# Two-place attention loads, branch sums in the other buffer, and a planner that counts accumulating transfers by other constants, in an encoder layer on one Trainium2 core

## The chip, the core and the metric

The kernel runs on one core of a Trainium2 chip. Time is device time of one execution in microseconds (us); lower is better. TensorE (PE) does the matmuls, VectorE (DVE) and ScalarE (ACT) the element-wise work, GpSimd (POOL) a few scalings and the accumulating transfers, and SyncE (SP) issues nearly all other transfers (DMAs). The five engines run their own instruction queues in order and wait for each other by semaphores. The profile also gives the clock that was granted to TensorE, as a share of full speed.

## The reference

One post-norm layer over 1024 frames of width 1024, float32 in and out:

```
proj = x @ w_in                                  # q,k,v (8 heads of 64), f_a, q_b,f_b,i_b,g_b, two gates
y_a = fox_attention(q, k, v, log_sigmoid(f_a))   # causal softmax(q.k/8 + F[t] - F[s]) @ v
y_b = rms_norm(hgrn2(silu(q_b), 1-f, i_b, log f)) * norm_g * sigmoid(g_b)   # linear recurrence
merged = sigmoid(gate_a) * (y_a @ w_pa) + sigmoid(gate_b) * (y_b @ w_pb)
x = layer_norm(ALPHA * x + merged @ w_o)
x = layer_norm(ALPHA * x + (silu(x @ w_g) * (x @ w_u)) @ w_ff_out)
```

## The kernel before

Float32 products are made from three matmuls of split operands (high by high, high by low, low by high), and the large products are cut by a Strassen-like scheme into seven block products p1 to p7. A matmul has 128 rows of weights and mostly 512 columns.

The layer runs in this order: the projections for v, the pairs of q/k and recurrence projections ("b" and "q" in the table ORDER), the recurrence heads ("r"), the early part of the gate projections ("e", products p3 and p7, parked in DRAM as `part_d`), the eight attention heads ("a") interleaved with the late parts of the eight gate pairs ("g"), then the two branch projections with the gates (`pps`), the output projection, the first norm, the feed-forward part and the second norm.

**Planner.** No engine's order is written by hand. The program is recorded call by call, ORDER giving the sequence of the large steps. A planner (class `Plan`) then simulates the engines with costs per instruction and searches for the order with the earliest end; that order is what each engine's queue holds on the chip. `cost` gives a transfer on SP its time from its bytes: 350 bytes per ns, but 235 where the SBUF side has 64 rows, and 220 where the first step of the source is 0. A transfer that POOL issues gets `LANDS` plus its bytes over `RATE` until it lands, and holds the modelled DMA for half of the latter part.

**Attention loads.** In `qk_load` a head's q and k come from DRAM (`qk_d`, split parts hi and lo) into three tiles of 128 rows: q2 holds 64 rows of hi above 64 rows of lo, k2 the hi part twice, kl the lo part twice. That is six transfers of 64 rows, 256 KB each. In `attention` a head's probabilities for late queries lie in a wide tile, in buffer m for even heads and buffer v for odd ones (`take("mv"[i], ...)`); POOL scales them by the reciprocal sums, TensorE transposes them (tile `pt`), ACT and DVE split the transposes (`th`, `tl`), and products with v are summed in `pv`, copied to `ya` and stored to `ya_d`.

**Branch sums.** After attention each of the four chunks (c = 0 to 3, heads 2c and 2c+1) of attention's output is fetched from `ya_d` in `branch_raw`: two heads, hi and lo, 64 rows each. Two plain loads on SP, then two accumulating transfers on POOL that add the lo part to what has landed. The chunks lie in `ybox[0]`, which is buffer v, so they wait for head 7's wide tile; sums and differences of them lie in `ybox[1]`, buffer m. ACT and DVE then split them into the operands y11, y12, y22, ys1 to ys4 of `pps`.

**Late gates.** `gate_late(n)` makes p1, p2, p6, p5, p4 with two PSUM banks, both of the group "h", so gate n+1's second product needs the bank that gate n's p4 leaves. That one is freed by a DVE addition `gl_b<-gl_h,gl_b`, whose second input is the parked p7 of gate n, loaded from `part_d` and used by one more addition before it.

Of the kernel before, what the change touches and what calls it, by code (L numbers as in the profile page):

```python
# [12 lines left out]
ALU = mybir.AluOpType  # L13
# [3 lines left out]
P = 128  # L17
S = 1024
D = 1024
KC = D // P  # L20
NT = S // P
HA, DH = 8, 64
# [8 lines left out]
FIRST = 8  # L31
WARM = 7
ROUNDS = 36
ORDER = ("b10 00", "b20 21", "b11 01", "r0", "q0", "b12 02", "r1", "b22 23", "q1", "r2", "b13 03", "q2", "e0", "r3", "q3", "e1",
         "e2", "e3", "e4", "e5", "e6", "e7", "a0", "a1", "g0", "a2", "a3", "g1", "a4", "g2", "a5", "a6", "g3", "a7", "g4", "g5", "g6", "g7")
MARGIN = 1.06
SLACK = 400.0
SWITCH = 300.0
# [23 lines left out]
class Plan:  # L62
# [2 lines left out]

    LAT = {"PE": 197.0, "ACT": 131.0, "DVE": 128.0, "POOL": 66.0, "SP": 2400.0}
    OWN = {"PE": 0.0, "ACT": 0.0, "DVE": 127.0, "POOL": 60.0, "SP": 2400.0}
    SOFT, LANDS, RATE = 950.0, 1050.0, 190.0
    SETS = {AF.Exp: 0, AF.Ln: 0, AF.Sigmoid: 1, AF.Silu: 2}

    def __init__(self, tc):
# [68 lines left out]
    def cost(self, eng, method, outs, ins, kw):  # L140
        o = outs[0]
        n = o.free_size()
        psum = any(str(a.space).endswith("PSUM") for a in ins)
        if eng == "PE":
            dt = ins[0].dtype
            if method == "transpose":
                return 109.0
            if dt == F32:
                return 2 * max(112.0, n / 1.2 + 2)
            return n / 2.4 + 13.4 if n > 128 else 111.0  # L150
        if eng == "ACT":
            d = n / 1.2 + (52 if psum else 94) + 95 * (o.partition_size() == DH)
            if "accum_out" in kw:
                d += 93
            return d + 93 * sum(isinstance(kw.get(x), bass.AP) for x in ("scale", "bias"))
        if eng == "DVE":
            scal = sum(1 for a in ins if a.free_size() == 1 and n > 1)
            two = method in ("tensor_scalar", "tensor_copy") and not psum
            if method == "reciprocal":
                return 90.0  # L160
            if method == "tensor_tensor_scan":
                return n * 2.1 + 69
            if method == "copy_predicated":
                return n * 1.3 + 69
            if method == "bn_stats":
                n = ins[0].free_size()
            return n * (0.5208 if two else 1.0417) + 69 + 61 * min(scal, 2)
        if eng == "POOL":
            if method == "dma_start":
                return self.SOFT  # L170
            if method == "tensor_tensor" and kw.get("op") == ALU.pow:
                return 500 + 260 * n
            if method == "tensor_scalar":
                return n * 0.833 + 244
            return n * 2.35
        near = ins[0] if str(o.space).endswith("DRAM") else o
        rate = 235.0 if near.partition_size() == DH else 220.0 if ins[0].ap[0][0] == 0 else 350.0
        return float(o.nbytes()) / rate

    def kind(self, call):  # L180
# [2 lines left out]
    def schedule(self, slack, wait):  # L183
# [13 lines left out]
        dma_free = 0.0  # L197
# [18 lines left out]
        while done < len(calls):  # L216
            best = None
            for q, av in avail.items():
                for i in av:
                    t = max(free[q], ready[i])  # L220
                    ok = True
                    need = {}
                    for name in calls[i][6]:
# [10 lines left out]
                        t = max(t, sorted(slots[tag])[k][0] + 60)  # L234
# [3 lines left out]
                    if self.lands[i]:  # L238
                        t = max(t, ring[-RING])
                    if q == "SP":  # L240
                        t = max(t, under_way[-8])
# [8 lines left out]
            t, _, i, q = best  # L250
            c = calls[i]
            avail[q].remove(i)
            d = c[7] * (1 if q in ("PE", "SP") else MARGIN)
# [3 lines left out]
            if q == "SP":  # L257
                start = max(t + 100, dma_free)
                dma_free = start + d
                free[q] = t + 480  # L260
                fin = dma_free
                under_way.append(fin + self.LAT["SP"])
            else:
                if q == "ACT":
                    kind = self.kind(c)
                    if kind is not None and kind != table:
                        table = kind
                        t -= wait
                        d += 1283
                free[q] = t + d  # L270
                fin = t + d + self.lands[i]
                if self.lands[i]:
                    fin += max(0.0, dma_free - t - d)
                    dma_free = max(dma_free, t + d) + 0.5 * (self.lands[i] - self.LANDS)
                    fin = max(fin, ring[-1] + self.lands[i] - self.LANDS)
                    ring.append(fin)
            self.times[i] = t
# [117 lines left out]
def trunk(ctx: ExitStack, tc, a: dict, out: bass.AP):  # L395
# [21 lines left out]
    def take(tag, shape, name, dt=F32):  # L417
        return plan.tile(root, [P] + shape, dt, tag, name, BUFS[tag])
# [26 lines left out]
    def f(ap):  # L445
        return ap.bitcast(F32)
# [91 lines left out]
    b11 = block(0, 0, ("kb", "kb"), "b11")  # L538
# [15 lines left out]
    for k, b, A, p, o in ((0, b11, A11, "p1", vx), (1, b21, A12, "p2", vy)):  # L554
        T = stationary4("v" + p)
        raw = rows(b)
# [160 lines left out]

    ya_d = dram.tile([4, 2, 2, DH, S], F32, name="ya_d")

    v_d = dram.tile([HA, P, NT, 2, DH], F32, name="v_d")  # L720
    for h in range(HA):
        two = take("qk", [NT, 2, DH], f"v{h}", F32R)
# [164 lines left out]
    def qk_load(h):  # L887
        p, i = divmod(h, 2)
        me = slice(i * DH, (i + 1) * DH)
        q2, k2, kl = full("qk", f"q2_{h}", F32R), full("kb", f"k2_{h}", F32R), full("kb", f"kl_{h}", F32R)  # L890
        for t, ns in ((q2, (0, 1)), (k2, (2, 2)), (kl, (3, 3))):
            for j, n in enumerate(ns):
                sync.dma_start(f(t)[j * DH:(j + 1) * DH], qk_d[p, n, me])
        return q2, k2, kl

    def attention(h):
# [251 lines left out]

    ZTAGS = ["kb"] * 4 + ["hl"] * 2 + ["qk"] * 2
    YTAGS = ["qk"] * 4 + ["pf"] * 4  # L1150
    ybox = [take(t, [4, S], f"ybox{t}") for t in "vm"]
    def operand(tag, name):
        t = take(tag, [2, 4, NB], name, F32R)
        return t[:, 0], t[:, 1]
# [20 lines left out]
    def branch_raw(i, c):  # L1175
        if i:
            return raw_load(yb_d[c], [S], f"yr{i}{c}")
        raw = ybox[0][:, c]
        for n in range(2):
            for j in range(2):  # L1180
                o = raw[j * DH:(j + 1) * DH]
                if n:
                    pool.dma_start(o, ya_d[c, j, n], accum_op=ALU.add)
                else:
                    sync.dma_start(o, ya_d[c, j, n])
        return raw

    def gated(i, fb, hf):
# [16 lines left out]
    for c in range(2):  # L1205
# [4 lines left out]
        t = y24[c]  # L1210
# [617 lines left out]
    return np.concatenate([t[:, :1], t[:, 1:, ::-1]], axis=1).reshape(S, D)  # L1828


def _layout(x, w_in, b_fgate, hgrn_lb_logits, hgrn_norm_g, w_branch_a, w_branch_b, w_out, ln1_g, ln1_b,
            w_ff_in, w_ff_out, ln2_g, ln2_b):
    c = np.ascontiguousarray
    x = _backwards(np.asarray(x)[0])
    w = np.asarray(w_in)[0]
    off = np.cumsum([0, 512, 512, 512, HA, 512, 512, 512, 512, D, D])

    def cols(i):
        return w[:, off[i]:off[i + 1]]

    def blocks(m):
        k, n = m.shape
        return m.reshape(k // P, P, n // P, P).transpose(2, 1, 0, 3)

    def pairs(m):
        k, n = m.shape
        return m.reshape(k // (2 * P), 2, P, n // NB, NB).transpose(3, 0, 2, 1, 4)

    def quarters(m):

        k, n = m.shape
        q = m.reshape(k // (2 * P), 2, P, 2, NB).transpose(1, 3, 0, 2, 4).reshape(4, k // (2 * P), P, NB)
        odd = q.shape[1] % 2
        q = np.concatenate([q, np.zeros_like(q[:, :odd])], axis=1)
        return c(q.reshape(4, -1, 2, P, NB).transpose(0, 1, 3, 2, 4))

    wff = np.asarray(w_ff_in)[0]
    return {
        "xT": c(x.T.reshape(KC, P, S)),
        "x": c(x),  # L1860
        "w_v": c(np.stack([cols(i).reshape(2, 4, P, NB) for i in (2, 6)], axis=1)),
        "w_f": c(cols(3).reshape(KC, P, HA).transpose(1, 0, 2)),
        "w_qk": c(np.stack([blocks(cols(0)), blocks(cols(1))])),
        "w_b": c(np.stack([blocks(cols(4)), blocks(cols(5)), blocks(cols(7))])),
        "w_g": c(np.stack([blocks(cols(8)), blocks(cols(9))])),
        "w_p": c(np.stack([blocks(np.asarray(v)[0]).reshape(4, 2, P, 4, P).transpose(0, 2, 1, 3, 4)
                           for v in (w_branch_a, w_branch_b)])),
        "w_o": c(pairs(np.asarray(w_out)[0])),
        "w_ff": c(np.stack([blocks(wff[:, :FF]), blocks(wff[:, FF:])], axis=1)),
        "w_fo": quarters(np.asarray(w_ff_out)[0]),  # L1870
        "bf": c(np.repeat(np.asarray(b_fgate)[0], NT).reshape(NT * HA, 1)),
        "lbl": c(np.asarray(hgrn_lb_logits)[0].reshape(HB, P).T),
        "ng": c(np.asarray(hgrn_norm_g)[0].reshape(P, 1)),
        "ln1c": c(np.concatenate([np.asarray(v)[0].reshape(KC, P).T for v in (ln1_g, ln1_b)], axis=1).reshape(P, 2, KC)),
        "ln1_g": c(np.asarray(ln1_g)[0]), "ln1_b": c(np.asarray(ln1_b)[0]),
        "ln2_g": c(np.asarray(ln2_g)[0]), "ln2_b": c(np.asarray(ln2_b)[0]),
    }
# [17 lines left out]
```

## Time and profile before

| what | value |
|---|---|
| median of 3 runs | 1408.5 us (1408.06 to 1409.1) |
| the profiled execution, its own time | 1405.97 us |
| its span, first to last instruction | 1404.1 us |
| TensorE busy | 1386.7 us, 99% |
| VectorE, ScalarE, GpSimd busy | 1151.3, 659.3, 97.6 us |
| granted TensorE clock, mean | 0.996 |
| moved by DMA | 252.51 MB, mean 180 GB/s |

All views are of the one profiled execution. "Waits" lists who waited for whom: total, number of times, longest. "Windows" gives for each stretch of the span the busy time of PE, PE's weight loads, DVE, ACT and POOL with the number of instructions, then the granted clock, the busy share of the DMA engines (which can read a little above 1) and GB/s. "Timeline" rows are start, duration, engine, line, operation, output<-inputs, and in brackets the engine's idle time before and what ended it. "DMA issues" rows are output<-input, issuing queue, count, KB each and median us from issue to landing, for the whole span or for those issued in a window. Names come without their numbers: `gl_b` is a tile of any late gate, `yboxv` the branch sums in buffer v, `p_w` a head's wide probabilities. All instructions have line 391, that of the planner's issue loop.

### The profile page before, as it was taken

Reading aid. Unit: us, or ns where it says so; the run is one execution under the profiler, and the core shown is the slowest. Engines: PE = TensorE matmul, PEld = TensorE weight load, DVE = VectorE, ACT = ScalarE, POOL = GpSimd, SP = SyncE. Lnnn points to the kernel's source line nnn. Section 1 sums busy time; section 2 is a strip of 40 time slices with the busy share of each in tenths; the row PEclk is TensorE's granted clock in tenths of the full one; section 3 lists DMA queues with packets and bytes.
Section 4 is the critical chain, followed back from the end, with each engine's and each line's share of the span. In section 5 each row is a group of like instructions: output and inputs, shape, how many; then the busy total and the mean of one; then the engine's idle time right before and its main releaser. Section 6 shows DMA issues by size and latency. Waiting matters only on the chain.

```text
span 1404.1 us, 19027 instructions
## 1 busy us (share of the span) xinstructions
PE 1386.7 (99%) x6578; PEld 1150.8 (82%) x6578; DVE 1151.3 (82%) x2026; ACT 659.3 (47%) x1207; POOL 97.6 (7%) x112
## 2 busy tenths in 40 slices
PE   9999999999999999899999999999999999999997
PEld 7788888888888888688887888888888888888886
DVE  8998898887589896798998889877687966888596
ACT  6545454444577575465549832233322334434330
POOL 0000100000124242000001000000000000000011
PEclk9999999999999999999999999999999999999999
DMA  7134343448899966756544636532224337977632
GB/s 273 38 148 160 105 136 128 158 150 277 263 305 295 265 201 189 232 173 224 196 150 135 218 108 225 170 120 101 95 105 135 113 113 234 356 254 231 216 118 83
DMA packets 104255, 252.51 MB, mean 180 GB/s; under 512 B 11984, under 2 KB 17232, under 8 KB 104160
## 3 DMA queue, kind: packets, MB, share of 16 engines
q1 hardware_dynamic: 102368, 245.01, 53.0%
q0 software_dynamic: 1792, 6.29, 2.3%
q8 instruction: 52, 0.85, 0.2%
q14 instruction: 43, 0.35, 0.1%
HBM read 184.87 MB, written 66.39 MB: 179 GB/s over the span
## 4 chain that ended last, share of the span: by engine, by line
PE 95%; DMA 3%; DVE 1%; issue 0%; ACT 0%; SPq 0%; DVEq 0%; ACTq 0%
PE p L391 15%; PE fb L391 12%; PE fc L391 9%; PE gl_h L391 6%; PE fa L391 5%; PE b_h L391 4%; PE b_s L391 4%; PE vx L391 4%; PE fe L391 3%; PE oa L391 3%; PE pps L391 3%; PE ge L391 3%; PE qk_s L391 3%; PE qk_h L391 3%; PE vy L391 3%; PE ob L391 2%
## 5 line engine op out<-in xcount | busy, mean ns | idle before, releaser
L391 PE MATMUL p<-dp 128*128 128x512 f32 (+1 forms) x957 | 210.1, 382 | 0.0
L391 PEld LDWEIGHTS p<-dp 128*128 128x128 f32 x957 | 175.1, 188 | 34.8
L391 PE MATMUL fc<-xs,Tp 128*128 128x512 f32 x528 | 128.9, 389 | 0.0
L391 PE MATMUL fb<-xs,Tp 128*128 128x512 f32 x528 | 127.8, 389 | 0.0
L391 PEld LDWEIGHTS fb<-xs,Tp 128*128 128x128 f32 x528 | 99.1, 188 | 20.6
L391 PEld LDWEIGHTS fc<-xs,Tp 128*128 128x128 f32 x528 | 99.1, 188 | 20.6
L391 ACT CAST Tp<-t 128x512 fp32r<-128x512 f32 x88 | 54.4, 620 | 127.7 <-PE fb L391 66.1
L391 DVE TENSOR_TENSOR Tp<-t,Tp 128x512 fp32r<-128x512 f32 x88 | 60.3, 688 | 29.8 <-ACT Tp L391 29.4
L391 PE MATMUL fa<-x,Tp 128*128 128x512 f32 x336 | 81.2, 389 | 0.0
L391 PEld LDWEIGHTS fa<-x,Tp 128*128 128x128 f32 x336 | 63.1, 188 | 13.1
L391 POOL TENSOR_TENSOR norm<-norm,few 128x1 f32<-128x1 f32 x16 | 13.5, 843 | 802.1 <-DVE norm L391 794.0
L391 ACT CAST dp<-dap 128x1024 fp32r<-128x1024 f32 (+1 forms) x42 | 41.0, 979 | 52.8 <-PE p L391 29.0
L391 DVE TENSOR_TENSOR dp<-dap,dp 128x1024 fp32r<-128x1024 f32 (+1 forms) x42 | 47.4, 1130 | 17.6 <-ACT dp L391 15.7
L391 DVE TENSOR_TENSOR tl<-pt,th 128x512 fp32r<-128x512 f32 (+1 forms) x96 | 52.5, 552 | 8.6 <-ACT th L391 4.5
L391 ACT CAST th<-pt 128x512 fp32r<-128x512 f32 (+1 forms) x96 | 45.7, 477 | 25.9 <-PE pt L391 22.9
L391 PE MATMUL fb<-x,Tp 128*128 128x512 f32 x240 | 57.6, 389 | 0.0
L391 PEld LDWEIGHTS fb<-x,Tp 128*128 128x128 f32 x240 | 45.0, 188 | 9.4
L391 DVE TENSOR_TENSOR u<-fb,p 128x512 f32<-128x512 f32 x40 | 27.6, 689 | 22.0 <-PE fb L391 21.9
L391 POOL TENSOR_SCALAR p_w<-p_w,sums 128x640 f32<-128x640 f32 (+3 forms) x32 | 37.7, 1203 | 36.0 <-DVE sums L391 36.0
L391 ACT CAST Tp<-wg_r 128x512 fp32r<-128x512 f32 x28 | 17.5, 623 | 47.1 <-PE fb L391 25.4
L391 ACT CAST dp<-chain 128x1024 fp32r<-128x1024 f32 (+1 forms) x18 | 17.7, 982 | 42.0 <-issue 21.5
L391 DVE TENSOR_TENSOR u<-fc,u 128x512 f32<-128x512 f32 x44 | 30.1, 685 | 7.1 <-PE fc L391 7.1
(1657 smaller groups left out, 3685.0 us busy)
## 6 DMA issues: line engine op xcount, KB each, us to landing
dbp<-in_w_fo SPq DMA_DIRECT2D x45, 512.0 KB, 4.8
dap<-a_d SPq DMA_DIRECT2D x35, 512.0 KB, 4.5
wg_r<-in_w_ff SPq DMA_DIRECT2D x22, 512.0 KB, 4.1
wu_r<-in_w_ff SPq DMA_DIRECT2D x22, 512.0 KB, 3.7
a_d<-ar SPq DMA_DIRECT2D x42, 256.0 KB, 3.2
wop_r<-in_w_o SPq DMA_DIRECT2D x18, 512.0 KB, 4.0
a_d<-as SPq DMA_DIRECT2D x33, 256.0 KB, 3.2
qk_d<-qk SPq DMA_DIRECT2D x32, 256.0 KB, 3.9
```

Of the source, the lines that this page charges most:

```text
L391: getattr(q.engine, method)(*args, **kw)
```

## The change

1. `qk_load` fetches each of the three tiles by one transfer of 128 rows. A new helper `twos` writes a source pattern that takes its rows in turn from two places: row 2d of the tile is row d of the first place, row 2d+1 row d of the second (step 0: the same place twice). The dot products run over all 128 rows, so their order is free.
2. `branch_raw` does the same with the two heads of a chunk: one load and one accumulating transfer a chunk, of 128 rows. `_by_twos` puts the rows of the branch weight in the same order on the host.
3. `ybox` is taken from "mv" and not from "vm": the chunks now lie in buffer m (free after head 6) and their sums in buffer v.
4. The planner: `LANDS` 1050 to 1950, `RATE` 190 to 238, a POOL transfer holds the modelled DMA for all of its transfer part, and the rate of 220 is used only for a source broadcast to 128 rows.
5. ORDER: b13 03 ahead of r2, e1 ahead of q3, g0 ahead of a1, g1 ahead of a3.

```
-ORDER = (... "q1", "r2", "b13 03", "q2", "e0", "r3", "q3", "e1",
-         "e2", ..., "a0", "a1", "g0", "a2", "a3", "g1", "a4", "g2", "a5", "a6", "g3", "a7", "g4", ...)
+ORDER = (... "q1", "b13 03", "r2", "q2", "e0", "r3", "e1", "q3", "e2", "e3",
+         ..., "a0", "g0", "a1", "a2", "g1", "a3", "a4", "g2", "a5", "a6", "g3", "a7", "g4", ...)
-    SOFT, LANDS, RATE = 950.0, 1050.0, 190.0
+    SOFT, LANDS, RATE = 950.0, 1950.0, 238.0
-        rate = 235.0 if near.partition_size() == DH else 220.0 if ins[0].ap[0][0] == 0 else 350.0
+        rate = 235.0 if near.partition_size() == DH else 220.0 if tuple(ins[0].ap[0]) == (0, P) else 350.0
-                    dma_free = max(dma_free, t + d) + 0.5 * (self.lands[i] - self.LANDS)
+                    dma_free = max(dma_free, t + d) + self.lands[i] - self.LANDS
+    def twos(ap, step):
+        return bass.AP(tensor=ap.tensor, offset=ap.offset, ap=[list(ap.ap[0]), [step, 2]] + [list(d) for d in ap.ap[1:]])
-        for t, ns in ((q2, (0, 1)), (k2, (2, 2)), (kl, (3, 3))):
-            for j, n in enumerate(ns):
-                sync.dma_start(f(t)[j * DH:(j + 1) * DH], qk_d[p, n, me])
+        for t, n, step in ((q2, 0, P * S), (k2, 2, 0), (kl, 3, 0)):
+            sync.dma_start(f(t), twos(qk_d[p, n, me], step))
-    ybox = [take(t, [4, S], f"ybox{t}") for t in "vm"]
+    ybox = [take(t, [4, S], f"ybox{t}") for t in "mv"]
-        for n in range(2):
-            for j in range(2):
-                ...
+        sync.dma_start(raw, twos(ya_d[c, 0, 0], 2 * DH * S))
+        pool.dma_start(raw, twos(ya_d[c, 0, 1], 2 * DH * S), accum_op=ALU.add)
+def _by_twos(w):
+    return w.reshape(4, 2, DH, D).transpose(0, 2, 1, 3).reshape(4 * P, D)
```

Every engine executes the same arithmetic as before; TensorE's queue holds the same numbers of matmuls of each width, in another order. 32 transfers fewer are issued (24 in attention, 8 for the branch sums). Three places of the queues matter below. In the names, `ya7_0` is head 7's first half of output, `gl5_b` a tile of late gate 5, `wg7_0` its raw weights, `s7` scores of head 7, `p7_w` its wide probabilities, `sums` its softmax sums; `yboxv`, `yboxm` are the branch chunks or sums in buffer v or m.

SP's queue at the end of attention, before:

```order
L391 DMA ya_d_177<-ya7_0_1246 128x512
L391 DMA yboxv_1350<-ya_d_177 64x1024 x4
L391 DMA gate_d_189<-gl4_b_1291 128x512
L391 DMA yboxv_1350<-ya_d_177 64x1024 x2
L391 DMA gate_d_189<-gl4_b_1291 128x512
L391 DMA yboxv_1350<-ya_d_177 64x1024
L391 DMA wg7_0_1334<-in_w_g 128x1024
L391 DMA gl5_b_1307<-part_d_190 128x512 x2
```

SP's queue now, around head 6's last store (`ya6_1`):

```order
L391 DMA gate_d_189<-gl3_a_1203 128x512
L391 DMA yboxm_1350<-ya_d_177 128x1x1024 x3
L391 DMA gate_d_189<-gl3_b_1204 128x512
L391 DMA ya_d_177<-ya6_1_1198 128x512
L391 DMA wg6_1_1319<-in_w_g 128x1024
```

And SP's queue now, from head 7's first store on:

```order
L391 DMA ya_d_177<-ya7_0_1246 128x512
L391 DMA gate_d_189<-gl4_b_1291 128x512 x2
L391 DMA gate_d_189<-gl4_a_1290 128x512
L391 DMA wg7_0_1334<-in_w_g 128x1024
L391 DMA gl5_b_1307<-part_d_190 128x512 x2
L391 DMA wg7_1_1335<-in_w_g 128x1024
L391 DMA gate_d_189<-gl5_a_1306 128x512
L391 DMA ya_d_177<-ya7_1_1285 128x512
L391 DMA gate_d_189<-gl5_b_1307 128x512
L391 DMA yboxm_1350<-ya_d_177 128x1x1024
L391 DMA wp0_1_r_1389<-in_w_p 128x1024
```

Three of the four chunks are fetched before head 6's last store instead of after head 7's first, and none stands between that store and gate 5's parked parts; the fourth now waits for the store of `ya7_1` two places ahead of it.

POOL's queue around the scaling of head 7's wide probabilities, before:

```order
L391 TENSOR_SCALAR p7_3_1230<-p7_3_1230,sums_1220 128x512
L391 TENSOR_SCALAR p7_w_1219<-p7_w_1219,sums_1247 128x640
L391 TENSOR_SCALAR p7_w_1219<-p7_w_1219,sums_1247 128x768
L391 TENSOR_SCALAR p7_w_1219<-p7_w_1219,sums_1247 128x896
L391 TENSOR_SCALAR p7_w_1219<-p7_w_1219,sums_1247 128x1024
L391 DMA yboxv_1350<-ya_d_177 64x1024 x8
```

POOL's queue there now:

```order
L391 TENSOR_SCALAR p7_3_1230<-p7_3_1230,sums_1220 128x512
L391 DMA yboxm_1350<-ya_d_177 128x1x1024 x3
L391 TENSOR_SCALAR p7_w_1219<-p7_w_1219,sums_1247 128x640
L391 TENSOR_SCALAR p7_w_1219<-p7_w_1219,sums_1247 128x768
L391 TENSOR_SCALAR p7_w_1219<-p7_w_1219,sums_1247 128x896
L391 TENSOR_SCALAR p7_w_1219<-p7_w_1219,sums_1247 128x1024
L391 DMA yboxm_1350<-ya_d_177 128x1x1024
```

ACT's queue in the same place now, from the exponential of head 7's last scores on:

```order
L391 ACTIVATE p7_w_1219,sums_1247<-p7_w_1219,soft_1257 128x1024
L391 CAST th7_0_2_1241<-pt7_0_2_1240 128x256
L391 CAST Tgl4p4h_1300<-wg4_0_1286 128x512
L391 CAST y12h_1358<-yboxm_1350 128x512
L391 CAST th7_0_3_1244<-pt7_0_3_1243 128x128
```

Three accumulating transfers now stand ahead of POOL's scaling of `p7_w`, and ACT reads the first of them (chunk 2, `y12h`) ahead of head 7's `th7_0_3`.

DVE's queue at the end of gate 6, now:

```order
L391 TENSOR_TENSOR gl6_b_1323<-gl6_a_1322,gl6_b_1323 128x512
L391 TENSOR_TENSOR tpa_0_1369<-wp0_0_r_1368 128x256
L391 TENSOR_TENSOR gl6_a_1322<-gl6_a_1322,gl6_b_1323 128x512
L391 TENSOR_TENSOR yboxv_1351<-yboxm_1350 128x512
L391 TENSOR_TENSOR gl6_b_1323<-gl6_h_1320,gl6_b_1323 128x512
```

The row on `yboxv_1351` adds chunks 1 and 3 and so needs the fourth chunk's accumulating transfer; before, a row on chunks fetched earlier stood in its place. The row behind it frees the bank that gate 7's second product uses.

More of the change, by code (lines that the diff above doesn't have):

```diff
@@ L33 @@
 ROUNDS = 36
-ORDER = ("b10 00", "b20 21", "b11 01", "r0", "q0", "b12 02", "r1", "b22 23", "q1", "r2", "b13 03", "q2", "e0", "r3", "q3", "e1",
-         "e2", "e3", "e4", "e5", "e6", "e7", "a0", "a1", "g0", "a2", "a3", "g1", "a4", "g2", "a5", "a6", "g3", "a7", "g4", "g5", "g6", "g7")
+ORDER = ("b10 00", "b20 21", "b11 01", "r0", "q0", "b12 02", "r1", "b22 23", "q1", "b13 03", "r2", "q2", "e0", "r3", "e1", "q3", "e2", "e3",
+         "e4", "e5", "e6", "e7", "a0", "g0", "a1", "a2", "g1", "a3", "a4", "g2", "a5", "a6", "g3", "a7", "g4", "g5", "g6", "g7")
 MARGIN = 1.06
@@ L1178, in branch_raw @@
         raw = ybox[0][:, c]
-        for n in range(2):
-            for j in range(2):
[L1181 to L1185, printed above, removed]
+        sync.dma_start(raw, twos(ya_d[c, 0, 0], 2 * DH * S))
+        pool.dma_start(raw, twos(ya_d[c, 0, 1], 2 * DH * S), accum_op=ALU.add)
         return raw
@@ L1865, in _layout @@
         "w_g": c(np.stack([blocks(cols(8)), blocks(cols(9))])),
-        "w_p": c(np.stack([blocks(np.asarray(v)[0]).reshape(4, 2, P, 4, P).transpose(0, 2, 1, 3, 4)
-                           for v in (w_branch_a, w_branch_b)])),
+        "w_p": c(np.stack([blocks(v).reshape(4, 2, P, 4, P).transpose(0, 2, 1, 3, 4)
+                           for v in (_by_twos(np.asarray(w_branch_a)[0]), np.asarray(w_branch_b)[0])])),
         "w_o": c(pairs(np.asarray(w_out)[0])),
```

## The prediction

> **What bounds the kernel now.** I read the page first, then the waits of TensorE, then the windows and the timeline around the one long wait.
>
> ```profile
> PE 1386.7 (99%) x6578; PEld 1150.8 (82%) x6578; DVE 1151.3 (82%) x2026; ACT 659.3 (47%) x1207; POOL 97.6 (7%) x112
> PE 95%; DMA 3%; DVE 1%; issue 0%; ACT 0%; SPq 0%; DVEq 0%; ACTq 0%
> ```
>
> TensorE is busy for 1386.7 of 1404.1 us and carries 95% of the chain that ended last. The change leaves its matmuls as they are, so time can only come from the stretches in which it waits or runs slowly. Its waits in all:
>
> ```profile
> PE gl_h L391 <- DVE gl_b L391: 6.6, 1, 6.6
> PE pv L391 <- ACT ya L391: 0.5, 1, 0.5
> PE s L391 <- DMA kl<-qk_d: 0.4, 1, 0.4
> PE gl_h L391 <- ACT Tgl0p1h L391: 0.3, 1, 0.3
> ```
>
> One wait of 6.6 us is nearly everything. The windows around it (engines' busy time, granted clock, DMA share, GB/s):
>
> ```profile
> 525.00:530.00 5.00, 5.00 (x28) 4.20 (x27) 4.91 (x18) 3.59 (x8) 0.44 (x1) 1.00 0.11 41
> 550.00:555.00 5.00, 5.00 (x24) 4.14 (x23) 1.98 (x3) 1.73 (x3) 1.68 (x2) 1.00 1.04 252
> 565.00:570.00 5.00, 2.48 (x11) 1.70 (x10) 0.00 (x0) 0.81 (x2) 0.00 (x0) 1.00 1.07 249
> 571.00:573.00 2.00, 0.00 (x0) 0.00 (x0) 0.90 (x3) 0.00 (x0) 0.00 (x0) 0.50 1.00 379
> 575.00:577.00 2.00, 2.00 (x6) 1.52 (x6) 2.00 (x4) 1.28 (x3) 0.00 (x0) 0.50 0.87 263
> ```
>
> At 525 the DMA engines are nearly idle; from 550 to past 570 they are full. The clock falls to 0.50 while TensorE stands and stays there beyond 575. The timeline of that stretch:
>
> ```profile
> 548.02 2.37 SPq L391 DMA_DIRECT2D yboxv<-ya_d  x4
> 551.11 0.68 DVE L391 TENSOR_TENSOR Tgl5p5l<-wg,Tgl5p5h 128x512 fp32r<-128x512 f32 x1
> 552.03 0.86 POOL L391 DMA_DIRECT2D yboxv<-ya_d  x1 [17.93 <-DMA yboxv<-ya_d]
> 554.58 1.35 SPq L391 DMA_DIRECT2D gl_b<-part_d  x2
> 562.60 0.32 SPq L391 DMA_DIRECT2D ya_d<-ya  x1
> 564.60 0.39 PE L391 MATMUL gl_h<-xh,Tgl6p1h 128*128 128x512 f32 x1
> 572.15 0.69 DVE L391 TENSOR_TENSOR gl_a<-gl_a,gl_b 128x512 f32<-128x512 f32 x1 [1.10 <-DMA gl_b<-part_d]
> 574.11 0.79 PE L391 MATMUL gl_h<-xh,Tgl6p2h 128*128 128x512 f32 x1 [6.63 <-DVE gl_b L391]
> 577.67 0.39 PE L391 MATMUL gl_h<-xh,Tgl6p2l 128*128 128x512 f32 x1
> ```
>
> Seven loads of chunks go out from 548, six accumulating transfers follow from 552, and gate 5's parked parts, issued at 554.58, queue with them. The chain says how long, and what a matmul costs at full clock:
>
> ```profile
> 555.62 16.45 DMA gl_b<-part_d
> 1166.86 2.72 PE fa L391 x12
> ```
>
> 16.45 us for 256 KB. DVE gets it at 572.15, frees the bank, and TensorE goes on at 574.11. From there to 577.67 it starts 8 matmuls in 3.56 us, where 8 x 2.72/12 = 1.81 would do.
>
> **The change, part by part.**
>
> *The wait removed.* 6.63 + (3.56 - 1.81) = 8.4 us, if gate 5's parts land in time. In the new queue of SP they stand behind `wg7_0`, whose buffer comes free with the split that ends at 551.8 (row 551.11), and the backlog is gone: three chunks of four, with their accumulating transfers, went out at about 524. So issue near 553. What 256 KB and 512 KB took, for transfers issued in quiet and in full stretches (for the first two the median of the whole span, then of windows):
>
> ```profile
> gl_b<-part_d SPq DMA_DIRECT2D x16, 256.0 KB, 8.0
> ya_d<-ya SPq DMA_DIRECT2D x16, 256.0 KB, 7.7
> ...
> box<-nf_d POOLq DMA_DIRECT2D x1, 512.0 KB, 5.1
> ...
> ya_d<-ya SPq DMA_DIRECT2D x1, 256.0 KB, 2.0
> ...
> yboxv<-ya_d POOLq DMA_DIRECT2D x6, 256.0 KB, 11.1
> ...
> wp_r<-in_w_p SPq DMA_DIRECT2D x2, 512.0 KB, 4.8
> ...
> ya_d<-ya SPq DMA_DIRECT2D x1, 256.0 KB, 12.6
> ```
>
> Even at the median of 8.0 the parts are there at 561. TensorE needs the bank one product after 564.60, at 567.3. Six us of room: **-8.4**.
>
> *The three early chunks.* They move into head 7's attention, ahead of POOL's scaling of its wide probabilities. The rows of that place:
>
> ```profile
> 523.59 0.69 POOL L391 TENSOR_SCALAR p<-p,sums 128x512 f32<-128x512 f32 x1 [1.70 <-PE pt L391]
> 528.91 0.27 PE L391 MATMUL pt<-ident,p_w 128*128 128x128 f32 x1
> 529.56 4.55 POOL L391 TENSOR_SCALAR p_w<-p_w,sums 128x640 f32<-128x640 f32 x4 [5.27 <-DVE sums L391]
> 531.45 1.15 ACT L391 ACTIVATE p_w<-p_w,soft 128x1024 f32<-128x1024 f32 x1
> 536.99 0.60 PE L391 MATMUL pt<-ident,p_w 128*128 128x128 f32 x4
> ```
>
> Before, the scaling ends at 534.1 and the first wide transposes start at 536.99: 2.9 us of room. I place the new events by counting columns along TensorE's queue, 512 to 0.227 us. Head 6's last transpose (528.91) comes 4.9 us earlier, so the loads issue at 524.0 and the first lands 4.8 later, 528.8. Head 7's narrow scores come 4.8 us later, so POOL ends their scaling at 523.59 + 0.69 + 4.8 = 529.1. Three issues at 0.86 and about 0.3 between (an estimate) last to 532.3. Head 7's last scores come 2.0 us later (nine times 512 columns less between them and the transposes), so the wide scaling, ready at 531.6, starts 0.7 late and ends at 536.9. Room: nothing. If the loads come late, all three issues (3.5 us) lie on the path; at best none. I take **+0.5**, nearer to the rows of the quiet stretch (DMA share 0.11).
>
> *ACT behind chunk 2.* ACT comes to `y12h` after that last exponential (ends 532.6, now 534.6) and two casts, by 536. The transfer issued at 529.1 lands 5.1 later if the engines are free (534.2), 11.1 later if they are as full as after 550 (540.2). Behind it ACT holds `th7_0_3` and a table load that TensorE already waited 0.5 for (the second wait). Bounds 0 and +4.2; **+0.5**, as three transfers share the engines, and not a backlog of thirteen.
>
> A page speaks against this move. The Trainium skill, "SBUF — State Buffer", section "SBUF: two separate sides", says that a DMA issued by GpSimd cannot get its descriptors written while VectorE runs an operation in a two-port mode, copies above all. If each issue lost one 0.69 us operation of VectorE to that, POOL would be 2.1 us later and the sum 1.6 higher. Against it stands an issue in attention with VectorE busy throughout:
>
> ```profile
> 504.08 0.91 POOL L391 DMA_DIRECT2D box<-nf_d  x1 [5.48 <-DMA box<-in_causal]
> ```
>
> It took 0.91 us beside 0.86 with VectorE mostly idle (row 552.03), so I add nothing.
>
> *The fourth chunk.* Its load waits for the store at 562.60 to land, its accumulating transfer for the load, and DVE's addition of it stands ahead of the one that frees gate 7's bank. Quiet: 562.6 + 2.0 + 4.8 + 5.1 + 0.5 of handing on (estimate) = 575.0. TensorE wants the bank after six products from 564.60, at 580.9, so DVE must start its two additions of 0.69 by 579.5. Room 4.5: **0**. With 12.6 and 11.1 in place of 2.0 and 5.1 it is 591.6, 12.1 late. SP is held at that load too; gate 6's parts behind it are wanted at about the same time and go out 567 to 570, which their 8.0 covers.
>
> *The attention loads.* 48 half-height transfers become 24: SP issues 24 fewer at about 0.5 us. SP's time is not on the path, and a DMA saving there is covered by TensorE's queue, busy but for the two short waits. Head 1's scores move back by some 16 us, so its wait on `kl` goes: **-0.4**. Gate 0 moves ahead of head 1. Its first weights take the buffer of the last early product's operand, and between that operand's last use and gate 0 there are now 1.3 us less of matmuls; the load there takes
>
> ```profile
> wg<-in_w_g SPq DMA_DIRECT2D x3, 512.0 KB, 6.4
> ```
>
> and was 0.3 late already. Bounds 0 and +1.3: **+0.8**, since the six transfers issued around it are shorter now. Elsewhere the order differs by a few matmuls at a time in stretches that showed no wait, and that stays 0; the last 700 us are nearly the same queue.
>
> Sum: 1405.97 - 8.4 + 0.5 + 0.5 - 0.4 + 0.8 = 1399.0 for an execution like the profiled one. That one stands 2.5 us under the median of the runs shown (1408.5), so I forecast **1401.5 us**, with 1399 to 1404 as its own range: the small terms at their better ends, or 2.5 us of them worse.
>
> **The rivals.**
>
> *The early chunks hold up attention.* For it: no room on POOL, and ACT's `y12h`. Against it: the DMA share of 0.11 just before. With chunk 2 at 540.2, TensorE stands 4.2 us more, and the clock costs 1.75 again: 1399.0 - 0.5 + 4.2 + 1.75 = 1404.5, in the median 1407.0, no change that can be told. The Trainium skill, "TensorE: Matmul & The Clock Gate", section "Part 1: The HAM clock gate (the "warmup" mystery)", has the clock fall after an idle stretch of about 3.4 us; by that a stall of 3 us would cost 3, not 4.75. The rows agree as far as they go: 0.50 after 6.63 us.
>
> *The wait moves to gate 7.* The fourth chunk at 591.6 by the loaded rows: a stall of 12.1 and 1.75 of slow clock, 1399.0 + 13.9 = 1412.9, in the median **1415.4, slower**. For it: three transfers in series in front of a bank's release, and 12.6 is what this very store took. Against it: that was the backlog. It decides against the change from 10 us of stall and clock, the chunk at 587.8.
>
> *The change doesn't do what it says.* If gate 5's parts are as late as before, by some other transfer in the same place, it is 1408.5. Against it: little else is issued between 545 and 553.
>
> **How the numbers follow.** A difference under 0.2% (2.8 us) can't be told from none here. Chances: forecast 0.62, held-up attention 0.15, moved wait 0.11, nothing done 0.12. Faster: 0.62 and a third of the second, 0.67. Same: the rest of the second and the fourth, 0.22. Slower: 0.11. The range, 1399.0 to 1409.0, takes in the second and fourth cases and leaves out the moved wait and the forecast's lower tail.
>
> **What would show it.** Right: no wait `gl_h <- gl_b`, clock 1.00 through 560 to 585, loads of `yboxm` issued near 524, POOL's first of them by 530, TensorE's waits together under 3 us. Wrong: a wait of TensorE on `pt` or `pv` near 537 (POOL or ACT held up), one on `gl_h` near 581 (the fourth chunk), or waits of some us in 380 to 400, where the heads' order changed.

## The result, and the profile after

The changed kernel took 1405.17 us (median of 11 executions, 1402.89 to 1406.99), the kernel before beside it 1409.1 us (one of its 11 executions read 4775.49 us; without it the median is 1408.8). The ratio is 0.9972, with a 95% interval of 0.9962 to 0.9982; measured a second time, with the last experiments, it was 0.9967 (0.9954 to 0.9980). So the change makes the kernel faster, by 3.6 to 4.6 us (the two pairs of medians lie 3.9 and 3.6 apart, the ratios give 3.9 and 4.6). The forecast was 7.0 us less: the sign was right, half to two thirds of the size came. The time lies outside the forecast's own range of 1399 to 1404, and within the wider one, which took in two rivals as well.

The page of the changed kernel, busy times and chain, then the four longest of its waits of TensorE (total, times, longest):

```profile
PE 1391.0 (99%) x6578; PEld 1152.1 (82%) x6578; DVE 1154.7 (82%) x2026; ACT 661.2 (47%) x1207; POOL 93.0 (7%) x108
PE 96%; DMA 2%; DVE 1%; issue 0%; POOL 0%; ACT 0%; SPq 0%; DVEq 0%; ACTq 0%
```

```profile
PE pv L391 <- ACT th L391: 2.2, 2, 1.7
PE vy L391 <- DVE idle L391: 1.2, 1, 1.2
PE pt L391 <- POOL p_w L391: 0.7, 1, 0.7
PE pps L391 <- DVE sg L391: 0.6, 1, 0.6
```

The wait of 6.6 us on `gl_b` is gone. In its place stands one of 1.7 us on `pv`, for a split `th` of ACT. The windows of the changed kernel (busy PE, weight loads, DVE, ACT, POOL, then granted clock, DMA share, GB/s) show where, and what it did to the clock:

```profile
535.00:540.00 5.00, 5.00 (x26) 4.03 (x25) 3.64 (x14) 4.82 (x11) 2.65 (x4) 1.00 0.99 343
540.00:545.00 5.00, 3.29 (x17) 2.40 (x16) 4.06 (x3) 1.29 (x4) 3.04 (x4) 1.00 1.08 249
545.00:550.00 5.00, 5.00 (x19) 4.00 (x20) 3.60 (x6) 4.89 (x9) 0.00 (x0) 0.66 1.03 279
565.00:570.00 5.00, 5.00 (x24) 4.14 (x23) 4.21 (x7) 1.25 (x4) 0.00 (x0) 1.00 0.54 197
```

From 565 to 570, where TensorE was busy for 2.48 us before, it works throughout. But between 540 and 545 it stands, and after that the clock is at 0.66. Its timeline there:

```profile
529.32 1.81 SPq L391 DMA_DIRECT2D yboxm<-ya_d  x3
533.98 0.99 POOL L391 DMA_DIRECT2D yboxm<-ya_d  x1 [1.21 <-PE s L391]
538.30 0.95 POOL L391 DMA_DIRECT2D yboxm<-ya_d  x1 [1.64 <-DMA yboxm<-ya_d]
543.71 0.62 ACT L391 CAST y12h<-yboxm 128x512 fp32r<-128x512 f32 x1 [3.90 <-DMA yboxm<-ya_d]
544.24 0.26 ACT L391 CAST th<-pt 128x128 fp32r<-128x128 f32 x1
544.55 0.33 PE L391 MATMUL pv<-th,vhl 128*128 128x128 f32 x1 [1.71 <-ACT th L391]
561.28 0.96 SPq L391 DMA_DIRECT2D gl_b<-part_d  x2
```

Chunk 2's accumulating transfer is issued at 533.98 and ACT's `y12h` goes on at 543.71, 9.7 us later. ACT stood for 3.90 us, the `th` behind it is late, and TensorE stands for 1.71.

**TensorE's extra time by stage.** To place small losses I take each matmul's time from its start to the next one's start, less the median of that for its shape (0.227 us for 512 columns), and add these up by stage, over all 6578 rows of TensorE. This is "extra time" in the expectations below; it holds waits and slow clock alike. In us, each kernel in its one profiled execution:

| stage of the span | before | changed | changed, again |
|---|---|---|---|
| 0 to 20 | 0.8 | 3.4 | 1.7 |
| 20 to 370 | 2.7 | 3.6 | 2.9 |
| 370 to 410 | 2.3 | 3.8 | 4.9 |
| 410 to 530 | 1.4 | 1.7 | 2.0 |
| 530 to 610 | 9.5 | 4.1 | 3.9 |
| 610 to the end | 0.6 | 1.7 | 0.7 |
| all | 17.3 | 18.2 | 16.2 |
| the execution's own time | 1405.97 | 1406.99 | 1405.03 |

Two stages move for a cause in the queues. 530 to 610 wins 5.4 to 5.6 us where the forecast had 7.4 (8.4 less twice 0.5), and 370 to 410, where the heads begin, loses 1.5 to 2.6 where it had 0.4. The two profiled executions of before and after lie 1 us the wrong way round: that of before was 2.5 us under its median, that of the changed kernel 1.8 above its own, 2.6 of that in its first 20 us, where TensorE's queue is the same in both.

### The profile page after: what moved, and what is told of

Read it like the earlier page. It is cut to its first block, busy times and chain, and to the rows that moved or that the text cites. A ratio compares the mean times of both kernels' runs of the same rounds, so it can differ in the third digit from the quotient of the medians.

```text
span 1405.1 us, 18981 instructions
## 1 busy us (share of the span) xinstructions
PE 1391.0 (99%) x6578; PEld 1152.1 (82%) x6578; DVE 1154.7 (82%) x2026; ACT 661.2 (47%) x1207; POOL 93.0 (7%) x108
## 4 chain that ended last, share of the span: by engine, by line
PE 96%; DMA 2%; DVE 1%; issue 0%; POOL 0%; ACT 0%; SPq 0%; DVEq 0%; ACTq 0%
PE p L391 15%; PE fb L391 12%; PE fc L391 9%; PE gl_h L391 7%; PE fa L391 5%; PE b_h L391 4%; PE b_s L391 4%; PE vx L391 4%; PE oa L391 3%; PE fe L391 3%; PE qk_s L391 3%; PE qk_h L391 3%; PE ge L391 3%; PE pv L391 2%; PE ob L391 2%; PE vy L391 2%
```

## The experiments

The question was where the missing 3 us went. Theory A: ACT, held by chunk 2's `y12h`. Theory B: POOL, late with the scaling of `p_w` behind three transfers. Later theory C took their place: the transfers' engines are full from 530 on, and whichever in-order queue comes first to an instruction that needs one of the transfers under way is held. All ratios are to the kernel before, timed beside each; a row has 5 to 12 executions of its kernel.

| kernel | median us | before, beside it | ratio (95%) |
|---|---|---|---|
| chunk 2's splits late | 1405.15 | 1408.7 | 0.9974 (0.9965 to 0.9983) |
| and the accumulations late | 1402.46 | 1408.7 | 0.9956 (0.9945 to 0.9968) |
| before, buffers swapped | 1402.8 | 1408.7 | 0.9965 (0.9951 to 0.9978) |
| changed, buffers not swapped | 1404.21 | 1408.7 | 0.9963 (0.9951 to 0.9976) |
| changed, ORDER of before | 1407.22 | 1408.51 | 0.9989 (0.9979 to 0.9999) |
| changed, six half loads a head | 1410.55 | 1408.51 | 1.0010 (1.0000 to 1.0019) |
| before, gate 5's parts first | 1409.09 | 1408.51 | 1.0003 (0.9992 to 1.0013) |
| before, ORDER of the change | 1409.97 | 1408.51 | 1.0008 (1.0000 to 1.0017) |
| before, whole loads | 1404.69 | 1407.65 | 0.9974 (0.9963 to 0.9986) |
| changed, ORDER of before, chunks behind the gates' loads | 1402.16 | 1407.65 | 0.9957 (0.9943 to 0.9971) |
| changed, again | 1404.06 | 1407.65 | 0.9967 (0.9954 to 0.9980) |

**1. Chunk 2's splits late.** The edit works on the planner's finished order: four instructions are put behind a later one, and all else stays.

```diff
-        order = self.improve(slack, wait)
+        order = self.behind_of(self.improve(slack, wait))
+    def behind_of(self, order):      # y12h, y22h (ACT), y12l, y22l (DVE) of chunk 2
+        last = self.at(order, "tl7_1_7", "tensor_sub", "DVE")[0]
+        ...
+        return self.put(order, sorted(set(picks)), last)
```

> The changed kernel, with the four splits of chunk 2 (y12h, y22h on ACT, y12l, y22l on DVE) placed behind head 7's last split; every other queue is as it was. Theory A, ACT is held by chunk 2: the stall of 1.7 us on pv at 542.8 and the 3.4 us of half clock behind it both go, TensorE's extra time between 540 and 550 falls from 4.0 to under 0.5 us, and the time is about 3.3 us under the changed kernel's (1401.9, ratio to before 0.9949). Theory B, POOL is late: p_w is still scaled behind three transfers until 543.0 and DVE's split beside it still ends at 543.6, so TensorE stands about 1 us between 541 and 546, on pt or on pv for tl; 1403 to 1405.

Neither theory held. The time stayed (1405.15), with a longer stall. Of this kernel, one row of TensorE's waits, and ACT's timeline:

```profile
PE pv L391 <- ACT ya L391: 2.5, 1, 2.5
```

```profile
540.25 0.62 ACT L391 CAST Tgl5p1h<-wg 128x512 fp32r<-128x512 f32 x1
545.62 1.28 ACT L391 ACT_TABLE_LOAD   x1 [4.74 <-DMA sg<-gate_d]
```

With `y12h` out of the way ACT ran to its next instruction that needs a transfer, the sigmoid of the gate `sg` with its table load, and stood there until 545.62. Theory A named the right engine and the wrong transfer; theory B's wait of 1 us on `pt` or `tl` is not there (0.3 is the longest). What `y12h` and `sg` share is the transfers' engines.

**2. The accumulations late too.** Added to the edit above:

```diff
+        scaled = self.at(order, "p7_w", "tensor_scalar", "POOL")[-1]
+        return self.put(order, [k for k in self.at(order, "yboxm", "dma_start", "POOL") if k < scaled], scaled)
```

> As the run before, and POOL's three accumulating transfers placed behind its scaling of head 7's wide probabilities. Theory A: nothing more than the run before gives, 1401.9. Theory B: only now does the stall go; about 1 us better than the run before, 1401.9 where that one is at 1403 or more, and DVE's split of 3.7 us beside the scaling starts later or is shorter. If the crowding of the transfers itself is the price, both stay at 1405.

The median is 1402.46, with executions from 1402.29 to 1403.29. Extra time between 530 and 610 fell from 4.1 to 1.4. The transfers issued from 529 to 545 (KB each, median us from issue to landing), of the changed kernel and then of this one:

```profile
sg<-gate_d SPq DMA_DIRECT2D x4, 256.0 KB, 11.8
gl_b<-part_d SPq DMA_DIRECT2D x2, 256.0 KB, 14.0
```

```profile
sg<-gate_d SPq DMA_DIRECT2D x4, 256.0 KB, 7.1
gl_b<-part_d SPq DMA_DIRECT2D x2, 256.0 KB, 7.6
```

Three accumulating transfers, 5 us later, and the same gate loads land in 7.1 us instead of 11.8. That is theory C: the accumulations were not late themselves in a way that mattered, they made others late. This and the run before differ in nothing else; between their medians lie 2.7 us. Whether it is the bytes of these transfers or the adding that fills the engines, the runs do not separate.

**3. Before, with the two buffers swapped, and the change without the swap.**

```diff
-    ybox = [take(t, [4, S], f"ybox{t}") for t in "vm"]
+    ybox = [take(t, [4, S], f"ybox{t}") for t in "mv"]
```

> The kernel before, with the buffers of the chunks and of their sums swapped and nothing else; the planner then fetches six of the eight half chunks behind head 6's early stores and leaves POOL's eight accumulating transfers behind the scaling of head 7's probabilities. If the swap alone removes the wait of 6.6 us for gate 5's parts: 8.4 us less than before, about 1400.5 (ratio 0.994), with no stall near 542. If the other parts of the change are needed for it (half the transfers, the planner's numbers): gate 5's parts still land late, TensorE stands 3 us or more for gl_b, and the time is 1404 or more.

> The changed kernel without the swap of buffers: the chunks lie in v and are fetched by three transfers of 128 rows behind head 7's first store, just ahead of gate 5's parts. If the backlog of chunk transfers made the wait of before, four loads in place of eight and the bytes unchanged leave most of it: a wait of 3 to 7 us for gl_b and slow clock, 1406 to 1409. If it was their number and not their bytes, the wait is under 1 us: 1401 to 1402.

Either alone does for the time what the whole change does: 1402.8 and 1404.21. The swap alone takes the wait on `gl_b` down to 0.6 us, and the crowd comes out on ACT, which waited for a gate (one row each of ACT's and TensorE's waits of that kernel):

```profile
ACT sg L391 <- DMA sg<-gate_d: 7.5, 1, 7.5
```

```profile
PE gl_h L391 <- ACT gl_a L391: 1.5, 1, 1.5
```

Without the swap, with three loads of 128 rows ahead of gate 5's parts, 1.9 us of that wait are left:

```profile
PE gl_h L391 <- DVE gl_b L391: 1.9, 1, 1.9
```

Both sides of the second expectation (3 to 7, under 1) missed it, and the time of the swap alone fell between the two of the first (1400.5, 1404 or more). What lowered the wait without the swap is not shown: the new ORDER alone, with loads of 64 rows, lowers it to 0.5 us (experiment 6). The early fetch, on which the forecast rests, is not needed for the gain. The extra time between 370 and 410 is far apart in these two, 0.9 us with the swap alone and 7.0 without it.

**4. Before, with gate 5's parts first.** The seven chunk loads on SP go behind the two loads of parts; a row of difference in SP's queue, none in the others'.

```diff
+        parts = self.at(order, "gl5_b", "dma_start", "SP")[1]
+        picks = sorted(k for q in ("SP", "POOL") for k in self.at(order, "yboxv", "dma_start", q) if k < parts)
+        return self.put(order, picks, parts)
```

> The kernel before with one change on SP: the seven loads of half chunks that stood ahead of gate 5's parked parts stand behind them, in the same stretch; all other queues as before. If the parts were late because of the transfers ahead of them, the wait of 6.6 us for gl_b and the slow clock behind it go: 8.4 us less, 1400.5 (ratio 0.994). If the parts wait for something else, or what is now late is the chunks' accumulation or the weights behind them, TensorE stands for that, 3 us or more, and the time is 1404 or more.

It won nothing: 1409.09. Its wait, and its timeline:

```profile
PE gl_h L391 <- DVE gl_b L391: 6.1, 1, 6.1
```

```profile
554.12 0.92 SPq L391 DMA_DIRECT2D gl_b<-part_d  x2
555.15 4.28 SPq L391 DMA_DIRECT2D yboxv<-ya_d  x7
572.21 0.69 DVE L391 TENSOR_TENSOR yboxm<-yboxv 128x512 f32<-128x512 f32 x1 [7.35 <-DMA yboxv<-ya_d]
572.82 0.68 DVE L391 TENSOR_TENSOR gl_b<-gl_a,gl_b 128x512 f32<-128x512 f32 x1
```

The parts go first and land in 4.6 us (16.45 before), and DVE is held all the same, now by the addition of chunks that stands ahead of `gl_b` in its queue: it runs at 572.21, where before it ran at 563.60 and the parts held DVE until 572.15. So the order of these loads only chooses which of the two is late; the stretch, with a DMA share of 0.96 to 1.07 from 555 to 575, is too full for both to come in time.

**5. The half loads.** The changed kernel, its queues as they are, with six transfers of 64 rows a head; then the reverse in the kernel before, one whole load at the place of each second half.

```diff
-        for t, n, step in ((q2, 0, P * S), (k2, 2, 0), (kl, 3, 0)):
+        for t, n, step, m in ((q2, 0, P * S, 1), (k2, 2, 0, 2), (kl, 3, 0, 3)):
+            plan.halves[len(plan.calls)] = [(f(t)[j * DH:(j + 1) * DH], qk_d[p, o, me]) for j, o in enumerate((n, m))]
...
-                getattr(q.engine, method)(*args, **kw)
+                [getattr(q.engine, method)(*v, **kw) for v in self.halves.get(i, [args])]
```

> The changed kernel with every queue as it is, but six transfers of 64 rows a head for q, k and kl in place of three of 128. If half-height transfers cost only the time of SP's queue, which nobody waits for: 1405 +- 1, within 0.1% of the changed kernel, with TensorE's extra time between 380 and 400 at 3 to 5 us. If the whole rows are worth time of their own: the loads land later, TensorE waits for kl or k in the stretch of the heads, and it is 1407 or more.

> The kernel before, every queue as it was, with one transfer of 128 rows for each of q, k and kl in place of two of 64. If whole rows are worth what the six halves cost in the changed kernel (5.4 us, 1410.55 against 1405.17): 1403 to 1405 (ratio 0.996 to 0.998), with TensorE's extra time between 370 and 530 lower, under 3 us, and the wait of 6.6 us for gl_b left as it is. If that cost came only with the changed order, in which gate 0's weights stand behind head 1's loads: within 1 us of the kernel before, 1407.5 to 1409.5.

The whole loads are worth 3.0 us in the kernel before (1404.69 against 1407.65) and 5.4 in the changed one (1410.55 against 1405.17, each in its own session; by the ratios 5.3). I had put them at nothing but the 0.4 us of `kl`. The first expectation's price for the halves came (1407 or more), but not its wait for `kl` or `k`: that kernel's waits are on `th`, `tl` and gate 0's weights. The one wait that stands in the kernel before with whole loads, beside the first one of the program, is the old one:

```profile
PE gl_h L391 <- DVE gl_b L391: 6.9, 1, 6.9
```

and the extra time between 370 and 410 is 0.8 us, where the kernel before had 2.3 in one execution and, with the same queues up to there, 3.7 in experiment 4. The windows show where this can come from. From 410 to 530, before, then before with whole loads, then changed, then changed with halves:

```profile
410.00:530.00 120.00, 120.00 (x688) 102.64 (x687) 108.89 (x327) 84.56 (x194) 43.45 (x51) 1.00 0.85 255
```

```profile
410.00:530.00 120.00, 120.00 (x688) 102.64 (x686) 108.84 (x329) 84.47 (x194) 44.22 (x51) 1.00 0.71 240
```

```profile
410.00:530.00 120.00, 120.00 (x695) 102.96 (x694) 110.11 (x336) 88.00 (x203) 45.05 (x55) 1.00 0.75 251
```

```profile
410.00:530.00 120.00, 118.31 (x685) 101.13 (x684) 107.99 (x328) 86.84 (x200) 44.60 (x54) 1.00 0.85 254
```

The share divided by the rate is 0.333 and 0.335 for 100 GB/s with halves (first and last), 0.296 and 0.299 with whole rows: a ninth less engine time for the same bytes, by estimate some 11 us of all sixteen engines here (0.85 x 120 x 0.11). From 380 to 400 they are full either way, and then the same shows as rate. Before, and before with whole loads:

```profile
380.00:400.00 20.00, 19.23 (x102) 15.47 (x101) 15.71 (x52) 15.78 (x36) 7.47 (x11) 1.00 1.03 301
```

```profile
380.00:400.00 20.00, 20.00 (x112) 17.05 (x111) 17.39 (x55) 16.92 (x38) 10.30 (x12) 1.00 0.99 348
```

The Trainium skill states this ("SBUF — State Buffer", section "Door 1: The DMA port swizzle (why `[64,N]` ≈ `[32,N]`)"): a transfer of 64 partitions uses half of the ports and gets little more than one of 32. The runs agree in direction, 301 against 348 GB/s with other transfers mixed in, and I had not weighed it.

The profiles place only a part of what the medians show: with whole loads 1.5 us less of extra time between 370 and 410 (2.9 against experiment 4) and 0.4 between 530 and 610; with halves in the changed kernel 1.7 to 2.0 us more between 410 and 530. The profiled execution of the halves was 2.8 us under its median, so the rest may lie in what one execution does not show. And the swap alone has only 0.9 us between 370 and 410 with halves, in a queue that the planner ordered anew, so whole loads are not the only way there.

**6. The table ORDER.** The changed kernel with the ORDER of before, and the kernel before with the new one.

```diff
-ORDER = (... "a0", "g0", "a1", "a2", "g1", "a3", ...)
+ORDER = (... "a0", "a1", "g0", "a2", "a3", "g1", ...)
```

> The changed kernel with the table ORDER of before. The planner then fetches three chunks behind head 6's first store, but leaves POOL's four accumulating transfers behind the scaling of head 7's probabilities, and ACT has no split of a chunk before the end of that head; gate 0 stands behind head 1 again. Theory: both losses of the changed kernel come with the new ORDER, 3.6 us of extra time between 380 and 400 against 2.1 before and 4.0 between 540 and 560 against 0.9 before; without it the first is under 2.1, the second under 1, and the time is 1399 to 1401 (ratio 0.993 to 0.995). Rival: the new ORDER is worth something elsewhere or the crowding of transfers around 540 comes back in another place: 1403 or more.

> The kernel before with the new table ORDER alone. SP's queue has four half chunks ahead of gate 5's parts now in place of seven. If the new ORDER costs time where gate 0 meets head 1: 3 us or more of extra time between 380 and 400, against 2.1 before; with a wait for gl_b of 3 to 7 us left, 1407 to 1411. If it is neutral there: 2 us in that stretch, and 1404 to 1407 by the shorter backlog.

For the stage of 370 to 410 the theory held: 2.5 us with the old ORDER, 3.8 and 4.9 with the new one, and 7.7 when the new ORDER stands in the kernel before. For the total it did not: 1407.22, because this order has ACT's other gates in the middle of head 7. One row of TensorE's waits, and one of ACT's timeline:

```profile
PE pv L391 <- ACT th L391: 4.3, 1, 4.3
```

```profile
551.56 1.22 ACT L391 ACTIVATE sg<-sg 128x512 f32<-128x512 f32 x2 [5.68 <-DMA sg<-gate_d]
```

The accumulations go out from 536 to 540 here, beside the second pair of gates; ACT is held for 5.68 us. The new ORDER in the kernel before saves nothing (1409.97): its wait on `gl_b` is down to 0.5 us, but 7.2 us of extra time remain between 530 and 610, 2.7 of them a wait for a gate's `gl_a` at 600, behind an addition of chunks on DVE, with slow clock after it.

**7. Chunks behind the gates' loads.** The kernel of the first run of 6, with the three early chunk loads on SP behind the fourth load of `sg` and gate 6's weights, and the edit of experiment 1.

```diff
+        n = max(raw, gate)           # SP: wg6_0, the fourth sg
+        picks = sorted(k for q in ("SP", "POOL") for k in self.at(order, "yboxm", "dma_start", q) if k < last)
+        return self.put(order, [k for k in picks if k < n], n)
```

> The changed kernel with the table ORDER of before, and with the three early loads of chunks placed on SP behind the four loads of gates (sg) and gate 6's weights, and the splits of chunk 2 behind head 7's last. If what held ACT was that transfers of chunks and of gates shared the engines: ACT's waits of 2.8 and 5.7 us for sg go below 1.5 together, TensorE's extra time between 530 and 610 falls from 8.9 to under 3 us, and the time is 1399 to 1402. If the crowd only moves on, to gate 5's parts or to the chunk additions on DVE: a wait of 2 us or more for gl_b, 1403 to 1407.

The median is 1402.16, the least of all, but by the ratio experiment 2 is its equal. The transfers issued from 529 to 545, and TensorE's longest waits:

```profile
sg<-gate_d SPq DMA_DIRECT2D x4, 256.0 KB, 4.9
gl_b<-part_d SPq DMA_DIRECT2D x2, 256.0 KB, 5.1
```

```profile
PE vy L391 <- DVE idle L391: 1.2, 1, 1.2
PE gl_h L391 <- DVE gl_a L391: 0.9, 2, 0.7
```

Against the first run of 6 only the place of three transfers and of four splits differs. ACT has no wait for `sg` left, TensorE's extra time between 530 and 610 falls from 8.9 to 1.2, and the ratio from 0.9989 to 0.9957, 4.5 us. With experiment 2 this bears theory C out for the stage.

**8. The changed kernel again.**

> The changed kernel as it is, beside the two above. Ratio to before 0.9972 +- 0.0012; its profile again with a stall on pv between 540 and 546 and an extra time of 3 to 5 us between 370 and 410.

As expected: 0.9967, a stall of 2.5 us on `pv`, 4.9 us of extra time between 370 and 410.

## Why the prediction was right in sign and too large

- **The wait removed, -8.4: right in the changed kernel.** No wait on `gl_b` above 0.2 us, clock 1.00 from 560 to 585. The changed kernel runs 5.2 us later than before by 530 (sum of the stage table), and the parts go out at 561.28, which is the forecast's 553 plus that and the stall with its clock; they landed in 4.7 us (8.0 taken). But the reason given, a backlog ahead of those two loads, was too narrow: experiment 4 took it away and won nothing, for the chunks were then late in their place.
- **The three early chunks, +0.5 for POOL: right in its times, not in its price.** Less the 5.2 us, the loads go out at 524.1 (forecast 524.0) and POOL's first issue is at 528.8 (529.1); the third waits for its load, and the scaling ends at 537.8 (536.9). TensorE never waited for it there. The issues took 0.95 to 0.99 us. VectorE ran no copy beside them, nor beside the issue at 504.08 on which the prediction left out the rule of starved descriptors; so the runs show no such loss here and do not test the rule.
- **ACT behind chunk 2, +0.5: the step that failed.** The landing had bounds of 534.2 and 540.2, on the time of before; it was 538.5. I took the value near the quiet end, for the DMA share of 0.11 between 525 and 530. The two rows behind that one, in the same view of the kernel before, were not weighed:

```profile
530.00:535.00 5.00, 5.00 (x29) 4.21 (x28) 3.44 (x9) 4.23 (x9) 4.11 (x4) 1.00 0.76 212
535.00:540.00 5.00, 5.00 (x30) 4.36 (x29) 2.50 (x6) 2.94 (x6) 0.00 (x0) 1.00 0.95 316
```

 The stretch into which the transfers were moved was already nearly full, with gates, parts and weights, and behind `y12h` the gate `sg` would have held ACT as long (experiment 1). The price was 1.7 us of stall and 1.5 of slow clock: the rival of held-up attention, given 0.15, at 1.7 us in place of its 4.2, since TensorE had products to run until 542.84, 3.0 us after ACT came to stand. In the second profile it was 2.5 us of stall and no slow clock.
- **The clock in that rival: a shorter stall was enough.** Here 1.71 us of standing was followed by a mean clock of 0.66 in the window from 545 to 550. By the rule of the Trainium skill that the prediction weighed ("TensorE: Matmul & The Clock Gate", section "Part 1: The HAM clock gate (the "warmup" mystery)"), an idle stretch of about 3.4 us, it would have cost nothing more; the measurement decides against it.
- **The fourth chunk, 0: right.** DVE adds it at 586.93 without a wait, and nobody waits for gate 7's bank.
- **The attention loads, -0.4: wrong in size.** Experiment 5 prices them at 3 to 5 us, and "covered by TensorE's queue" was not so between 370 and 410, where the engines are full and the waits for `kl` and gate 0's weights go with whole loads. That the rest is engine time too is argued from the windows and not shown.
- **Gate 0 ahead of head 1, +0.8 within 0 to 1.3: too small.** With whole loads the stage has 0.8 us of extra time in the order of before, 2.5 and 2.7 in the changed kernel with the ORDER of before (experiments 6 and 7), and 3.8 to 4.9 with the new ORDER (both profiles of the changed kernel and experiments 1 and 2; 7.0 without the swap): 1.1 to 4.1 for the move, and up to 6.2 with that last one. What bounds it is not only the weights: TensorE waits there for `th`, `tl` and `p_w` in turn. That head 1's scores no longer fill in would fit this; no run tests it.
- **Moved wait and nothing done:** did not happen in the changed kernel. In experiment 4 the parts came early, and the same bank was late for the chunks.
- **The signs.** Of the signs of being right, the wait on `gl_h`, the clock from 560 to 585 and the chunks' loads came; TensorE's waits together did not, at 5.5 us and not under 3. Two signs of being wrong came: the wait on `pv` near 537 (542 here), and 3.6 us of extra time from 380 to 400 (2.1 before).

The errors had opposite signs: 3 to 5 us of saving by the loads that I did not price, against 1.7 + 1.5 - 0.5 = 2.7 of loss behind chunk 2 and some 0.3 to 5.4 at gate 0 beyond the 0.8 taken. That the time came within 4 us of the forecast is in part the luck of these meeting. And the gains of the parts are in part the same gain: the swap alone (0.9965), the change without the swap (0.9963), whole loads alone (0.9974) and all together (0.9972 and 0.9967) are alike within their intervals. The runs show two reasons, that the early chunks give back in head 7 what they win behind it, and the new ORDER at 370 to 410 what the loads win there; whether these are all stays open.

## What to carry to other kernels

Before transfers are moved earlier, read the DMA share of the stretch that they move into, not of the one ahead of it, and list which in-order queues meet an instruction there that needs any transfer: in the full stretch here the first of them paid, whoever's transfer it was. When a waiting instruction is moved out of the way and the next one of its queue waits instead, the cause is what both wait on, and moving instructions one by one only hands the wait on. With loads of 64 rows among them the transfers here took an eighth more engine time for the same bytes (0.333 against 0.296), though nobody waited for the queue that issues them; price that where the engines are full.

## What the runs showed of the hardware that was not expected

- **Short stalls can halve the clock.** In the profiles of all these kernels, six idle stretches of TensorE of 1.4 to 1.8 us had no slow clock with them; of eight between 1.9 and 2.9 us, six had; the four of 4.4 us and more all had. (Idle is counted from start to start here, 1.86 for the wait of 1.71.) In the clock's records the six are slow stretches at 0.50, four of 3.41 us and two of 6.83, that begin between 1.2 us before the stall's end and 1.8 us after it; those of the four long stalls last 6.83. Two more of 3.41 us followed two stalls of 0.7 and 0.8 to 0.9 us close together, in the second profile of the changed kernel and in experiment 1. So by these figures a stall of 2 us cost 2 here, or some 3.5 to 5.
- **A run of POOL's scalings can hold a DVE operation throughout.** The same split, in the changed kernel, in experiment 1 and in experiment 2:

```profile
539.85 3.74 DVE L391 TENSOR_TENSOR Tgl4p4l<-wg,Tgl4p4h 128x512 fp32r<-128x512 f32 x1
```

```profile
539.50 3.08 DVE L391 TENSOR_TENSOR Tgl4p4l<-wg,Tgl4p4h 128x512 fp32r<-128x512 f32 x1
```

```profile
538.02 0.71 DVE L391 TENSOR_TENSOR Tgl4p4l<-wg,Tgl4p4h 128x512 fp32r<-128x512 f32 x1
```

 In the first two POOL scaled four tiles without a gap (to 543.04 and 542.03), and the split ended 0.55 us after the last. In the third it started 0.14 us ahead of POOL's fourth scaling, and that one took 1.56 us in place of the 1.13 of experiments 6 (first run) and 7. The Trainium skill ("SBUF — State Buffer", section "SBUF: two separate sides") has VectorE and GpSimd share a port pair that whoever starts first holds for a whole instruction; the rows fit that, and add that the other can be kept out for a whole run of instructions. It need not be: in the kernel before, the same split beside the same four scalings, also recorded without a gap, took 1.02 us and came between the second and the third. It was held in the four profiles in which the accumulating transfers stand right ahead of the scaling (3.08 to 3.74 us); why is open. In the changed kernel TensorE had no wait on a `tl` there.
